# A decoder layer on one core: first weights through ACT's queue, gamma scaled on POOL, a scratch column for the shifted variance

## The chip, the core and the metric

The kernel runs on one core of a Trainium2 chip. A core has engines that run side by side, each on its own in-order stream of instructions: TensorE (PE; its weight loads are listed as PEld), VectorE (DVE), ScalarE (ACT), GpSimd (POOL) and SyncE (SP), which here only issues DMA transfers. ACT and POOL can issue transfers too, each on a queue of its own; an issue stands in the same stream as the engine's other instructions. Engines wait for each other and for transfers by semaphores.

The metric is device microseconds of one execution. The kernel before took 662.29 us in the median of three runs (661.71 to 663.59). All times inside an execution are counted from the first instruction that the profile shows.

## The reference

One decoder layer on x of 512 tokens by 1024 channels, float32:

```python
proj = h @ w_in[l]
q, k, v, p, g = jnp.split(proj, [...], axis=-1)
y_attn = moba_attention(q.reshape(hs), k.reshape(hs), v.reshape(hs), rel_bias) @ w_branch_attn[l]
y_pool = multiscale_pool(p, w_pool_group[l], pool_scale[l]) @ w_branch_pool[l]
gates = jax.nn.sigmoid(g.astype(jnp.float32)).astype(h.dtype).reshape(B, S, N_BRANCHES, D)
mixed = gates[:, :, 0] * y_attn + gates[:, :, 1] * y_pool
h = layer_norm(ALPHA * h + mixed @ w_out[l], ln1_g[l], ln1_b[l])
a, u = jnp.split(h @ w_ffn_in[l], 2, axis=-1)
a = causal_dwconv(a, conv_w[l], conv_b[l])
f = (jax.nn.gelu(a, approximate=False) * u) @ w_ffn_out[l]
h = layer_norm(ALPHA * h + f, ln2_g[l], ln2_b[l])
```

`layer_norm` is `(x - mean) * rsqrt(var + 1e-5) * gamma + beta` over the 1024 channels of a token.

## The kernel before, in words

**Three matmuls for one.** Every float32 operand is split into a high part (rounded to the format that TensorE multiplies at full rate) and the low remainder, and a product is three matmuls: high by high, high by low, low by high (`mm3`, L144 to L148). `split` (L63 to L68) does this: ACT copies the source into `hi` (L67), or another copy that is passed in does; then DVE subtracts, `lo = src - hi` (L68).

**The weight stream.** Weights come in chunks of 128 by 1024 (512 KB). `fetch` (L92) takes the next chunk: a DMA on SP's queue into one of three `wraw` buffers (L108), then the split into one of five pairs `whi`, `wlo`. The first chunk alone is fetched in two halves of 512 columns (`early`), each with its DMA and split, and between the halves the second half of the first tile of x is loaded. `weights(i)` runs three chunks ahead of the matmuls.

**The head.** ACT has a dummy activation (L164) so that its table is loaded early; POOL sets `eps_t`, which the dummy reads; DVE clears a tile, and TensorE runs eight dummy matmuls on it (`WARM`, L168). Meanwhile x, transposed, comes in eight tiles of 128 by 512 (`load_x`, L171), the first in two halves whose high parts are made by DVE (L65, `nc.vector.tensor_copy`). The first real matmuls are those of v (L240), 12 for each of the eight tiles of x; a weight chunk serves two of these tiles.

**The middle.** Then follow the other input projections with attention and pooling between them, the branch projections (for each of eight channel tiles `f`, POOL adds the two gated branches, `mt`, L437, and the sum is split into `mx_hi`, `mx_lo`), the output projection (`wo`), the first layer norm, and the gated MLP's input matmuls (`fi`).

**The end.** The MLP's output matmul is done as seven products of half-size blocks (Strassen-like; `product`, L664, in the order of `PRODUCTS`). Some products read weight sums, which a DMA from POOL's queue accumulates into `tw` (L134); two read plain weights (`wraw`, L128). The last products are followed by the second layer norm, one row tile of 128 tokens after the other: `scale_out` for tiles 0 and 1, `share_out` for 2, `finish` for 3.

**Layer norm.** `ln_rows` (L447) loads gamma and beta, each copied to all 128 partitions (one DMA of 1 MB on POOL's queue, L449), and ACT multiplies gamma by -0.5 in place (L450). It is called for the first norm (L454) and for the second (L709); there the tile takes the place of another one (`ra`) and two DMAs on SP's queue then write beta into rows of `out` (L711). `moments` (L470): DVE's per-256-column statistics `st` (six numbers each) are aggregated to mean and variance in `mv` (L472), ACT takes the square root of variance plus epsilon (L473), and DVE adds epsilon to the variance in place (L474). `centre` computes `(x - mean) * (-0.5 gamma)` (L485). `invert` makes `1/sqrt` with one Newton step from both (L479 to L481), and its result scales the row (L489 and ACT).

**Order.** The program is written in the order above, but the order of the instructions on each engine is chosen when the kernel is built, by a planner that works with estimated durations; it is fixed afterwards. `finish` pins part of its DVE instructions in the written order.

Of the kernel before, what the change touches and what calls it, by code (L numbers as in the profile page):

```python
# [10 lines left out]
AF = mybir.ActivationFunctionType  # L11
ALU = mybir.AluOpType
# [15 lines left out]
EPS = 1e-5  # L28
# [3 lines left out]
LEAD = 3  # L32
RING = 5
TMP = 4
WARM = 8
NKEEP = 12
NLATE = 4
KH = NF // 2
# [5 lines left out]
def layer_kernel(ctx: ExitStack, tc: tile.TileContext, xT, x, w_v, w_c, rel_bias, invcnt, w_group,  # L44
                 pscale, w_br, w_out, lnr, w_fi, convp, w_fo, out):
    nc = tc.nc
# [9 lines left out]
    def bank(name):  # L56
        return ps.tile([P, S], F32, tag="ps", name=name)
# [5 lines left out]
    def split(hi, lo, src, copy=None):  # L63
        if copy:
            copy(hi, src)  # L65
        else:
            nc.scalar.activation(hi, src, AF.Copy)  # L67
        nc.vector.tensor_tensor(lo, src, hi.bitcast(F32), op=ALU.subtract)  # L68
# [9 lines left out]
    chunks = [w_v[c] for c in range(4)]  # L78
# [13 lines left out]
    def fetch(pool=None, early=None):  # L92
        i = state["next"]
        state["next"] = i + 1
        if isinstance(chunks[i], tuple):
            ready[i] = fetch_fo(i, *chunks[i])
            return
        raw = wp.tile([P, D], F32, tag="wraw", name=f"wraw{i}", bufs=3)
        if pool is None:
            hi = wp.tile([P, D], F32R, tag="whi", name=f"whi{i}", bufs=RING)  # L100
            lo = wp.tile([P, D], F32R, tag="wlo", name=f"wlo{i}", bufs=RING)
        else:
            hi = pool.tile([P, D], F32R, name=f"whi{i}")
            lo = pool.tile([P, D], F32R, name=f"wlo{i}")
        parts = 2 if early else 1
        for c in range(parts):
            sl = slice(c * (D // parts), (c + 1) * (D // parts))
            nc.sync.dma_start(raw[:, sl], chunks[i][:, sl])  # L108
            split(hi[:, sl], lo[:, sl], raw[:, sl])
            if c == 0 and early:  # L110
                early()
        ready[i] = (hi, lo)
# [7 lines left out]
    def fetch_fo(i, name, c):  # L120
        sl = piece(c)
        n = sl.stop - sl.start
        step = {"T3": "=B11", "B11": "+B12", "T1": "+B22", "T2": "+B21", "T4": None}
        if name in step:
            raw = tw[:, sl]
        else:
            raw = wp.tile([P, D], F32, tag="wraw", name=f"wraw{i}", bufs=3)[:, :n]
            nc.sync.dma_start(raw, half(name, sl))  # L128
        hi = wp.tile([P, D], F32R, tag="whi", name=f"whi{i}", bufs=RING)[:, :n]
        lo = wp.tile([P, D], F32R, tag="wlo", name=f"wlo{i}", bufs=RING)[:, :n]  # L130
        split(hi, lo, raw)
        then = step.get(name)
        if then and then[0] == "+":
            nc.gpsimd.dma_start(raw, half(then[1:], sl), accum_op=ALU.add)  # L134
        elif then:
            nc.sync.dma_start(raw, half(then[1:], sl))
        return hi, lo

    def weights(i):
        while state["next"] <= min(i + LEAD, state["limit"]):  # L140
            fetch()
        return ready[i]
# [6 lines left out]

    def split3(v, a):  # L150
        return tuple(t.rearrange("p (a c) -> p a c", a=a) for t in v)

    xT_hi = act.tile([P, KT, S], F32R, tag="actT_hi", name="xT_hi")
    xT_lo = act.tile([P, KT, S], F32R, tag="actT_lo", name="xT_lo")
# [12 lines left out]
    wb_ = bank("warm_ps")  # L167
    for i in range(WARM):  # L168
        nc.tensor.matmul(wb_, warm[:, :P], warm, start=True, stop=True)
# [5 lines left out]
    for kt in range(KT):  # L175
        xr = aw.tile([P, S], F32, tag="tmp", name=f"xr{kt}", bufs=TMP)
        if kt == 0:
            load_x(kt, xr, slice(0, 256), nc.vector.tensor_copy)
            fetch(early=lambda: load_x(kt, xr, slice(256, 512), nc.vector.tensor_copy))
        else:  # L180
            load_x(kt, xr)
            if kt % 2 == 0:
                fetch()
# [44 lines left out]
    for kt in range(KT):  # L228
        wh, wl = split3(weights(kt // 2), 2)
        wh, wl = wh[:, kt % 2, :], wl[:, kt % 2, :]  # L230
        xs_ = [(xT_hi[:, kt, j * P:(j + 1) * P], xT_lo[:, kt, j * P:(j + 1) * P]) for j in range(NT)]
        last = kt == KT - 1
        if last:
            for j in range(NT):
                mm3(bs[j], xs_[j], (wh, wl), False, True)
                nc.scalar.activation(vv[:, j, :], bs[j], AF.Copy)
        else:
            for n, (a, b) in enumerate(((0, 0), (1, 0), (0, 1))):
                for j in range(NT):
                    nc.tensor.matmul(bs[j], xs_[j][a], (wh, wl)[b], start=kt == 0 and n == 0, stop=False)  # L240
# [55 lines left out]
    def in_tile(n):  # L296
        kind, j = order[n]
        wh, wl = split3(weights(C0 + n), KT)
        b = bank(f"{kind}{j}")
        for kt in range(KT):  # L300
            mm3(b, (wh[:, kt, :], wl[:, kt, :]), (xT_hi[:, kt, :], xT_lo[:, kt, :]), kt == 0, kt == KT - 1)
        if kind == "q":
            q_done(j, b)
        elif kind == "k":
            k_done(j, b)
        elif kind == "p":
            pool_in(j, b)
        elif len(gslot) < NKEEP:
            gslot[j] = gates[:, len(gslot), :]
            nc.vector.tensor_copy(gslot[j], b)  # L310
        else:
            gslot[j] = late[:, len(gslot) - NKEEP, :]
            nc.scalar.activation(gslot[j], b, AF.Sigmoid)
# [106 lines left out]
    for f in range(KT):  # L420
# [7 lines left out]
        for br in (1, 0):  # L428
            b = bank(f"br{f}_{br}")
            for k in range(4):  # L430
                src = (zT_hi[:, k, :], zT_lo[:, k, :]) if br else (oT_hi[:, k, :], oT_lo[:, k, :])
                mm3(b, (wh[:, 4 * br + k, :], wl[:, 4 * br + k, :]), src, k == 0, k == 3)
            t = bp.tile([P, S], F32, tag="m", name=f"m{f}_{br}", bufs=4)
# [13 lines left out]
    def ln_rows(r):  # L447
        t = hw.tile([P, 2, D], F32, tag="lnb", name=f"lnb{r}")
        nc.gpsimd.dma_start(t, bass.AP(tensor=lnr.tensor, offset=lnr.offset + r * D, ap=[[0, P], [D, 2], [1, D]]))  # L449
        nc.scalar.activation(t[:, 0, :], t[:, 0, :], AF.Copy, scale=-0.5)  # L450
        return t

    lnb = ln_rows(0)
    ypool = ctx.enter_context(tc.tile_pool(name="ypool", bufs=1, reuse_waits="tile"))  # L454
    ytiles = [ypool.tile([P, S], F32, name=f"y{j}") for j in range(2)]
# [4 lines left out]
    st = const.tile([P, NT, 4, 6], F32, name="st")  # L460
# [9 lines left out]
    def moments(i):  # L470
        mu, var = mv[:, i, 0:1], mv[:, i, 1:2]
        nc.vector.bn_aggr(mv[:, i, :], st[:, i].rearrange("p a b -> p (a b)"))  # L472
        nc.scalar.activation(rstd[:, i, 0:1], var, AF.Sqrt, bias=eps_t)  # L473
        nc.vector.tensor_scalar(var, var, EPS, None, op0=ALU.add)  # L474
        return mu, var

    def invert(i, var, pin=lambda ins: ins):
        r, t = rstd[:, i, 0:1], rstd[:, i, 1:2]
# [14 lines left out]
    def scale_out(i):  # L493
        mu, var = moments(i)
        centre(i, slice(0, D), mu)
        r = invert(i, var)
        nc.scalar.activation(xs[:, i, :], xs[:, i, :], AF.Copy, scale=r)
        nc.gpsimd.dma_start(out[i * P:(i + 1) * P, :], xs[:, i, :], accum_op=ALU.add)

    def share_out(i):  # L500
        mu, var = moments(i)
        centre(i, slice(0, D), mu)
        r = invert(i, var)
        nc.scalar.activation(xs[:, i, right], xs[:, i, right], AF.Copy, scale=r)
        rescale(i, left, r)
        nc.gpsimd.tensor_tensor(xs[:, i, right], xs[:, i, right], lnb[:, 1, right], op=ALU.add)

    def finish(i):
        pin = tc.keep_in_program_order
        mu, var = moments(i)  # L510
        pin(centre(i, right, mu))
        r = invert(i, var, pin)
        nc.scalar.activation(xs[:, i, rest], xs[:, i, rest], AF.Copy, scale=r)
        pin(centre(i, left, mu))
        nc.gpsimd.tensor_tensor(xs[:, i, rest], xs[:, i, rest], lnb[:, 1, rest], op=ALU.add)
        pin(rescale(i, left, r))
        pin(rescale(i, most, r))
# [106 lines left out]
    for j in range(RING, 2 * NF):  # L624
        hb[j] = bank(f"fi{j}")
        fi_mm(j, hb[j], slice(0, S))
        if j % 2:
# [3 lines left out]
            if f % 2 == 0 and f >= 6 and f < 6 + 2 * NC:  # L631
                c = f // 2 - 3
# [74 lines left out]
    gather(3, S, D, bank_a[1], 1, False, False)  # L707
    product(5, bank_d, False)
    lnb = ln_rows(2)  # L709
    for i in range(2):  # L710
        nc.sync.dma_start(out[i * P:(i + 1) * P, :], lnb[:, 1, :])  # L711
# [89 lines left out]
```

## Time and profile before

| | us |
|---|---|
| median of three runs | 662.29 |
| the profiled execution, whole | 663.32 |
| its span, first to last instruction | 661.6 |
| TensorE busy in it | 649.4 |
| VectorE busy | 384.4 |
| ScalarE busy | 285.9 |
| GpSimd busy | 89.3 |
| DMA, mean | 127 GB/s, 83.70 MB |

How to read the rows that follow. A row of the timeline has the start and the duration in us, the engine (with a q behind it: the issue of a DMA or another sequencer instruction), the line, the operation, what it writes and reads, and how many were merged; in brackets is how long its engine had been idle before it, and what ended that. A row of the chain of waits has start, duration and what the chain ran through; a DMA there lasts from issue to landing. A row of the groups has the count, then busy us, mean ns of one, and idle us before them. A row of the waits has who waited for whom, the sum in us, how often and the longest. A row of DMA issues has the count, the size of each, and the median us to landing. A row of a stretch has its bounds and length, busy us of each engine in the order PE, PEld, DVE, ACT, POOL, the granted clock, the share of the DMA engines' time, and GB/s. A busy TensorE is not a TensorE at its peak, since the ends of matmuls are modelled and overlap the next ones.

### The profile page before, as it was taken

Reading aid. Unit: us, or ns where it says so; the run is one execution under the profiler, and the core shown is the slowest. Engines: PE = TensorE matmul, PEld = TensorE weight load, DVE = VectorE, ACT = ScalarE, POOL = GpSimd, SP = SyncE. Lnnn points to the kernel's source line nnn. Section 1 sums busy time; section 2 is a strip of 40 time slices with the busy share of each in tenths; the row PEclk is TensorE's granted clock in tenths of the full one; section 3 lists DMA queues with packets and bytes.
Section 4 is the critical chain, followed back from the end, with each engine's and each line's share of the span. In section 5 each row is a group of like instructions: output and inputs, shape, how many; then the busy total and the mean of one; then the engine's idle time right before and its main releaser. Section 6 shows DMA issues by size and latency. Waiting matters only on the chain.

```text
span 661.6 us, 8020 instructions
## 1 busy us (share of the span) xinstructions
PE 649.4 (98%) x3083; PEld 538.8 (81%) x3083; DVE 384.4 (58%) x559; ACT 285.9 (43%) x395; POOL 89.3 (14%) x137
## 2 busy tenths in 40 slices
PE   8999999999999999999999999999999999999994
PEld 6888787877888888889988888888888888888874
DVE  5556665554532675398456344443534548788596
ACT  5646556675422332232443333333323236555452
POOL 0705261211000124002100000000000001124002
PEclk9999999999999999999999999999999999999998
DMA  8643222222322227208942222233233334989905
GB/s 285 215 150 118 80 79 80 73 74 79 96 95 96 93 98 291 91 1 292 251 157 97 96 95 96 95 100 101 99 97 97 104 100 97 211 188 203 261 1 127
DMA packets 24918, 83.70 MB, mean 127 GB/s; under 512 B 3240, under 2 KB 3496, under 8 KB 24624
## 3 DMA queue, kind: packets, MB, share of 16 engines
q1 hardware_dynamic: 19312, 63.77, 29.1%
q0 software_dynamic: 5280, 18.90, 13.2%
q8 instruction: 24, 0.39, 0.2%
q10 hardware_dynamic: 288, 0.52, 0.2%
q14 instruction: 14, 0.11, 0.1%
HBM read 80.01 MB, written 3.17 MB: 126 GB/s over the span
## 4 chain that ended last, share of the span: by engine, by line
PE 77%; issue 10%; DMA 4%; POOL 4%; DVE 3%; ACT 1%; POOLq 0%; DVEq 0%; SPq 0%; ACTq 0%
PE fi L147 11%; PE fi L146 11%; PE fi L148 11%; PE g L146 4%; PE g L147 4%; PE g L148 4%; PE v L240 3%; PE wo L146 2%; PE br L147 2%; PE br L146 2%; PE wo L147 2%; PE wo L148 2%; PE br L148 2%; POOL tw L134 2%; PE ob L372 1%
## 5 line engine op out<-in xcount | busy, mean ns | idle before, releaser
L68 DVE TENSOR_TENSOR wlo<-wraw,whi 128x1024 fp32r<-128x1024 f32 (+1 forms) x105 | 134.3, 1284 | 119.8 <-ACT whi L67 117.9
L67 ACT ACTIVATE whi<-wraw 128x1024 fp32r<-128x1024 f32 (+1 forms) x105 | 109.0, 1041 | 187.4 <-PE fi L147 84.0
L147 PE MATMUL fi<-hT_lo,whi 128*128 128x512 f32 (+1 forms) x392 | 143.8, 367 | 0.0
L148 PE MATMUL fi<-hT_hi,wlo 128*128 128x512 f32 (+1 forms) x392 | 143.8, 367 | 0.0
L146 PE MATMUL fi<-hT_hi,whi 128*128 128x512 f32 (+1 forms) x392 | 143.5, 368 | 0.0
L148 PEld LDWEIGHTS fi<-hT_hi,wlo 128*128 128x128 f32 x392 | 73.9, 189 | 12.3
L147 PEld LDWEIGHTS fi<-hT_lo,whi 128*128 128x128 f32 x392 | 73.9, 189 | 12.0
L146 PEld LDWEIGHTS fi<-hT_hi,whi 128*128 128x128 f32 x392 | 73.6, 189 | 12.2
L134 POOL DMA_DIRECT2D tw<-in_w_fo x18 | 15.8, 906 | 269.9 <-DVE wlo L68 269.9
L146 PE MATMUL g<-xT_hi,whi 128*128 128x512 f32 x128 | 50.3, 393 | 0.0
L148 PE MATMUL g<-xT_hi,wlo 128*128 128x512 f32 x128 | 49.9, 390 | 0.0
L147 PE MATMUL g<-xT_lo,whi 128*128 128x512 f32 x128 | 49.8, 389 | 0.0
L67 ACT ACTIVATE whi<-tw 128x1024 fp32r<-128x1024 f32 (+1 forms) x30 | 29.4, 983 | 25.4 <-PE fi L147 11.3
L578 DVE TENSOR_TENSOR fT<-y,fi 128x512 f32<-128x512 f32 x22 | 15.1, 687 | 40.0 <-PE fi L148 39.2
L68 DVE TENSOR_TENSOR wlo<-tw,whi 128x1024 fp32r<-128x1024 f32 (+1 forms) x30 | 33.3, 1126 | 8.6 <-ACT whi L67 8.4
L577 ACT ACTIVATE y<-y 128x512 f32<-128x512 f32 x22 | 13.9, 632 | 43.0 <-DVE y L576 43.0
L148 PEld LDWEIGHTS g<-xT_hi,wlo 128*128 128x128 f32 x128 | 24.0, 188 | 5.1
L146 PEld LDWEIGHTS g<-xT_hi,whi 128*128 128x128 f32 x128 | 24.0, 188 | 5.0 <-issue 0.2
L147 PEld LDWEIGHTS g<-xT_lo,whi 128*128 128x128 f32 x128 | 24.0, 188 | 4.8
L345 POOL TENSOR_SCALAR pp<-pp,rs 128x128 f32<-128x128 f32 (+3 forms) x32 | 21.8, 698 | 37.7 <-PE g L148 18.4
L146 PE MATMUL wo<-whi,mx_hi 128*128 128x512 f32 x64 | 25.0, 390 | 0.0
L148 PE MATMUL wo<-whi,mx_lo 128*128 128x512 f32 x64 | 24.9, 389 | 0.0
(202 smaller groups left out, 1169.7 us busy)
## 6 DMA issues: line engine op xcount, KB each, us to landing
wraw<-in_w_fi SPq DMA_DIRECT2D x44, 512.0 KB, 3.3
wraw<-in_w_c SPq DMA_DIRECT2D x28, 512.0 KB, 3.4
tw<-in_w_fo POOLq DMA_DIRECT2D x20, 512.0 KB, 7.6
tw<-in_w_fo SPq DMA_DIRECT2D x10, 512.0 KB, 3.9
wraw<-in_w_fo SPq DMA_DIRECT2D x10, 512.0 KB, 5.2
wraw<-in_w_br SPq DMA_DIRECT2D x8, 512.0 KB, 3.3
wraw<-in_w_out SPq DMA_DIRECT2D x8, 512.0 KB, 3.4
strip<-F_d POOLq DMA_DIRECT2D x8, 256.0 KB, 3.5
```

The lines of the kernel that those rows point to most:

```text
L67: nc.scalar.activation(hi, src, AF.Copy)
L68: nc.vector.tensor_tensor(lo, src, hi.bitcast(F32), op=ALU.subtract)
L134: nc.gpsimd.dma_start(raw, half(then[1:], sl), accum_op=ALU.add)
L146: nc.tensor.matmul(out_, wh, ah, start=start, stop=False, **kw)
L147: nc.tensor.matmul(out_, wh, al, start=False, stop=False, **kw)
L148: nc.tensor.matmul(out_, wl, ah, start=False, stop=stop, **kw)
L240: nc.tensor.matmul(bs[j], xs_[j][a], (wh, wl)[b], start=kt == 0 and n == 0, stop=False)
L345: nc.gpsimd.tensor_scalar(pp[:, offs[i]:offs[i] + n], pp[:, offs[i]:offs[i] + n], rs[:, i:i + 1], 1.0, op0=ALU.mult, op1=ALU.mult)
L372: nc.tensor.matmul(b[e * DH:(e + 1) * DH, kb * P:], vv[:, kb, h * DH:(h + 1) * DH], PTs[h][:, toff[kb]:toff[kb] + n], start=kb == 0, stop= ...
L577: nc.scalar.activation(y, y, AF.Gelu)
L578: nc.vector.tensor_tensor(fT[:, j, :], y, u, op=ALU.mult)
```

## The change

Four things are changed:

1. One dummy matmul fewer (`WARM` 8 to 7).
2. The two halves of the first weight chunk are loaded by DMAs on ACT's queue, no longer SP's. The high part of the first half is made by two engines: DVE copies columns 0 to 191 and ACT columns 192 to 511. The second half is split as before.
3. Gamma is multiplied by -0.5 on POOL, no longer on ACT, at both calls of `ln_rows`.
4. Variance plus epsilon goes into the first number of the row tile's statistics, which are not read again after the aggregate, no longer over the variance itself.

```diff
-WARM = 8
+WARM = 7
...
-            nc.sync.dma_start(raw[:, sl], chunks[i][:, sl])
-            split(hi[:, sl], lo[:, sl], raw[:, sl])
+            (nc.scalar if early else nc.sync).dma_start(raw[:, sl], chunks[i][:, sl])
+            split(hi[:, sl], lo[:, sl], raw[:, sl], fast if early and c == 0 else None)
...
+    def fast(hi, src):
+        for copy, c in ((nc.vector.tensor_copy, slice(0, 192)), (first_copy, slice(192, 512))):
+            copy(hi[:, c], src[:, c])
+
+    def first_copy(hi, src):
+        nc.scalar.activation(hi, src, AF.Copy)
...
-        nc.scalar.activation(t[:, 0, :], t[:, 0, :], AF.Copy, scale=-0.5)
+        nc.gpsimd.tensor_scalar(t[:, 0, :], t[:, 0, :], -0.5, None, op0=ALU.mult)
...
-        nc.vector.tensor_scalar(var, var, EPS, None, op0=ALU.add)
-        return mu, var
+        shifted = st[:, i, 0, 0:1]
+        nc.vector.tensor_scalar(shifted, var, EPS, None, op0=ALU.add)
+        return mu, shifted
```

## The prediction

> **What bounds the kernel now.** I read the page's busy shares first, then who TensorE waited for, then the first 14 us, the last 60 us, and the gamma steps.
>
> ```profile
> span 661.6 us, 8020 instructions
> PE 649.4 (98%) x3083; PEld 538.8 (81%) x3083; DVE 384.4 (58%) x559; ACT 285.9 (43%) x395; POOL 89.3 (14%) x137
> ...
> PE warm_ps L169 <- DVE warm L166: 1.3, 1, 1.3
> PE v L240 <- ACT whi L67: 0.7, 1, 0.7
> PE fod L147 <- DVE wlo L68: 0.7, 1, 0.7
> ```
>
> TensorE is the bound: 649.4 of 661.6 us busy, and the three longest of its waits sum to 2.7 us. The change removes no matmul but one dummy, so it can gain only before the first matmul, after the last one, in the 0.7 us ahead of `fod`, and where matmuls run slowly. The head:
>
> ```profile
> 0.81 1.28 ACT L164 ACT_TABLE_LOAD   x1 [0.81 <-PEq L793]
> 1.25 0.42 SPq L108 DMA_DIRECT2D wraw<-in_w_v  x1
> 1.25 3.63 DMA wraw<-in_w_v
> 1.27 3.59 PE L169 MATMUL warm_ps<-warm 128*128 128x512 bf16 x8 [1.27 <-DVE warm L166]
> 2.10 0.20 ACT L164 ACTIVATE dummy<-eps_t 128x1 f32<-128x1 f32 x1
> 3.05 0.29 DVE L65 CAST xT_hi<-xr 128x256 fp32r<-128x256 f32 x1 [1.84 <-DMA xr<-in_xT]
> 4.91 0.63 ACT L67 ACTIVATE whi<-wraw 128x512 fp32r<-128x512 f32 x1 [2.60 <-DMA wraw<-in_w_v]
> 5.59 1.22 PE L240 MATMUL v<-whi,xT_hi 128*128 128x512 f32 x2 [0.73 <-ACT whi L67]
> 6.62 1.05 PE L240 MATMUL v<-whi,xT_lo 128*128 128x512 f32 x2
> 7.47 1.05 PE L240 MATMUL v<-whi,xT_hi 128*128 128x512 f32 x2
> 9.18 0.62 PE L240 MATMUL v<-whi,xT_lo 128*128 128x512 f32 x2
> 9.97 1.06 ACT L67 ACTIVATE whi<-wraw 128x1024 fp32r<-128x1024 f32 x1 [1.35 <-DMA wraw<-in_w_v]
> 11.02 1.07 PE L240 MATMUL v<-whi,xT_lo 128*128 128x512 f32 x4
> 11.92 1.07 PE L240 MATMUL v<-wlo,xT_hi 128*128 128x512 f32 x4
> ```
>
> (Start, duration, engine.) The first half chunk of weights is issued at 1.25, lands 3.63 us later, takes 0.63 us on ACT, and the first real matmul starts at 5.59; x was ready at 3.34. Matmuls start (7.47-6.62)/2 = 0.425 us apart until about 9.17, and (11.92-11.02)/4 = 0.225 apart after it. The stretch 5.59 to 9.17 thus runs at about half speed, and costs 3.58 x (1 - 0.225/0.425) = 1.68 us.
>
> **Part 1, first weights on ACT's queue, split by two engines.** An issue holds SP for 0.42 us (second row); the weights were second. On ACT they can go at 0.81, where that engine's stream began: 0.44 us earlier, if the issue precedes the table load (ready without a wait, while the dummy waits for `eps_t`). Transit to landing is unknown for this queue: the lower end is x's first slice, 3.05-0.82 = 2.23 us with nothing ahead; the upper is 3.63, this transfer behind that slice. I take 3.63, since the same 384 KB must move by then. Then the split: ACT's rows give 0.63 us for 512 columns and 1.06 for 1024, 0.84 ns each, so 320 columns cost 0.63 - 192 x 0.00084 = 0.47. DVE's 192 columns cost less than its 0.29 us for 256, and run beside ACT's. That saves 0.16. First matmul: 5.59 - 0.44 - 0.16 = 4.99, **0.60 us earlier**. The low end of the gain is below nothing (table load first, a rival below); the high end is 5.59-4.43 = 1.16, because the warm-up then stands in the way: one dummy fewer ends it at 4.86 - 0.43 = 4.43. That removed dummy saves nothing by itself and leaves an idle gap of 0.56 instead of 0.73.
>
> Also moved: SP loses two issues, so the x tiles and the second weight chunk go about 2 x 0.42 = 0.84 us sooner. That chunk's `whi` (11.03) has cover: TensorE reaches it after the eight matmuls of the last two rows, near 12.8. With the second half chunk issued late on ACT, say at 2.73, cover remains: landing 3.63 us later and split in 0.63, it would be ready at 7.0; it is used after twelve matmuls, about 9.18 + 4 x 0.225 = 10.1. I take the slow stretch to shift along with its start.
>
> The Trainium skill (DMA: Bandwidth & Descriptors, "Queues, rings and completion order") says that each DMA engine alternates between the queues that have work. By that rule x, now next on SP, shares with the weights, and these end after 512 KB rather than 384; this trace never has both queues at work, so it cannot confirm it. What that gives is a rival below.
>
> **Part 2, gamma on POOL.**
>
> ```profile
> L345 POOL TENSOR_SCALAR pp<-pp,rs 128x384 f32<-128x384 f32 x8 | 8.6, 1069 | 0.0
> L345 POOL TENSOR_SCALAR pp<-pp,rs 128x512 f32<-128x512 f32 x8 | 6.5, 816 | 0.0
> ...
> 251.82 0.54 POOL L449 DMA_DIRECT2D lnb<-in_lnr  x1
> 253.91 1.28 POOL L437 TENSOR_TENSOR mt<-m,m 128x512 f32<-128x512 f32 x1 [1.56 <-DVE m L434]
> 262.31 2.14 POOL L437 TENSOR_TENSOR mt<-m,m 128x512 f32<-128x512 f32 x1 [7.12 <-DVE m L434]
> 265.14 0.69 DVE L68 TENSOR_TENSOR mx_lo<-mt,mx_hi 128x512 fp32r<-128x512 f32 x1 [1.85 <-ACT mx_hi L67]
> 278.23 1.37 DVE L466 SCALAR_TENSOR_TENSOR xs<-xs,wo 128x512 f32<-128x512 f32 x2 [8.83 <-PE wo L148]
> ...
> DMA to landing us min/median/max: 8.2/9.2/10.6
> ```
>
> ACT loses two passes over 1024 columns (about 1.05 us each); POOL gains two, of 2 x 0.816 = 1.6 to 1.069 x 1024/384 = 2.9 us. They also make POOL wait for a landing of up to 10.6 us (last row). The first could hold the two mixing adds behind it: landing 251.8+10.6 = 262.4, scaled by 265.3, then adds, ACT, DVE: the last `mx_lo` moves from 265.8 to at most about 271. The last twelve `wo` matmuls that need it end when DVE resumes at about 278.2, so start near 275.5: hidden.
>
> The second:
>
> ```profile
> 613.95 1.06 ACT L450 ACTIVATE lnb<-lnb 128x1024 f32<-128x1024 f32 x1 [4.25 <-DMA lnb<-in_lnr]
> 632.18 1.06 ACT L67 ACTIVATE whi<-tw 128x1024 fp32r<-128x1024 f32 x1 [0.36 <-PE fod L148]
> ...
> 613.88 1.73 SPq L711 DMA_DIRECT2D out<-lnb  x2
> 618.37 3.74 SPq L128 DMA_DIRECT2D wraw<-in_w_fo  x3
> ...
> tw<-in_w_fo POOLq DMA_DIRECT2D x5, 512.0 KB, 10.7
> out<-lnb SPq DMA_DIRECT2D x2, 512.0 KB, 9.4
> ...
> 618.37 8.18 DMA wraw<-in_w_fo
> 633.48 0.50 PE fod L147
> ```
>
> ACT stood 4.25 us for gamma; behind it were `sd_hi`, `whi`, and so the weight buffer that SP refills at 618.37, whose landing at 626.55 leads to the 0.7 us stall at 633.48. Freed, ACT could let that load go at 613.88+1.73 = 615.6. But the two 512 KB beta stores of SP are ahead in the same queue and take 9.4 us to land, to about 625. The load's end follows them, whenever it is issued. So the ends are 0 and 0.7; I take **0**, as the row of 8.18 us says that this load queued rather than travelled. On POOL the `tw` additions behind gamma can be held until 613.9 + 2.9 = 616.8; the first then lands near 616.8+10.7 = 627.5, and ACT reads that piece at 632.18: hidden with 4.7 us left.
>
> **Part 3, the dead column.**
>
> ```profile
> 653.58 0.26 DVE L472 BATCH_NORM_AGGREGATE mv<-st 128x2 f32<-128x24 f32 x1
> 653.87 0.30 ACT L473 ACTIVATE rstd<-mv,eps_t 128x1 f32<-128x1 f32 x1 [1.77 <-DVE mv L472]
> 654.20 0.15 DVE L474 TENSOR_SCALAR mv<-mv 128x1 f32<-128x1 f32 x1 [0.36 <-ACT rstd L473]
> 654.27 0.74 DVE L485 SCALAR_TENSOR_TENSOR xs<-xs,mv,lnb 128x512 f32<-128x512 f32 x1
> ```
>
> In the last row tile, epsilon is added in place, so DVE idles 0.36 us until ACT has read the variance, with the centring, inverse and final scaling queued behind and no matmul left. Written elsewhere, the add follows the aggregate at once; the square root, done at 654.17, is still ahead of the reciprocal, which comes after 0.74 us of centring. Gain **0.36 us**; bounds 0 and 0.36. The other seven row tiles lie under matmuls.
>
> **Sum.** 0.60 + 0 + 0.36 = 0.96 us. The profiled execution took 663.32, 1.72 around its span and 1.03 above the median 662.29; on it the sum gives 662.36, on the median 661.33: **661.3 us**.
>
> **Rivals.**
> - *The slow stretch ends early* (chance 0.27). In the trace full speed came 3.58 us after the end of the idle gap (5.59), not after the first dummy (1.27). If the first weights land so early that the gap closes or is too short to count, 1.27+3.58 = 4.85 could end it, and the 1.68 us go too: 0.60+1.68+0.36 = 2.64, **659.7**. Against it: I leave 0.56 us of gap; and TensorE would want the second chunk at 12.8-2.3 = 10.5, before the `whi` at 11.03 if that comes no sooner. The Trainium skill (TensorE: Matmul & The Clock Gate, "Part 1: The HAM clock gate") says that full clock follows a window of about 3.4 us of sustained activity, and that the windows run freely; the 3.58 agrees, and a drifting start of windows would also vary from run to run.
> - *The stall goes as well* (0.15): 0.96+0.7 = 1.66, **660.6**. For it, 2.8 us earlier issue; against, the beta stores ahead.
> - *Shared engines* (0.13). The extra 128 KB ahead, at the rate just after (row below), cost 0.42 us and eat the earlier issue: 0.16-0.42+0.44+0.36 = 0.54, **661.8**.
> - *Slower: the issue stands behind ACT's table load* (0.10). ACT's first activation ends at 2.30; weights issued there instead of at 1.25 lose 1.05, less 0.16 and 0.36: **662.8**. It decides from an issue later than 1.25+0.16+0.36 = 1.77. For it: the dummy is ahead in the program; against: it needs `eps_t` first.
>
> ```profile
> 4.86:5.59 0.73, 0.00 (x0) 0.00 (x0) 0.31 (x2) 0.63 (x1) 0.00 (x0) 1.00 0.92 313
> ```
>
> (128 KB at the last column's 313 GB/s is 0.42 us.)
>
> **Numbers.** The forecast has 0.30, an unforeseen order of the work the last 0.05. The range reaches from below the early-clock case (with the stall gone as well it would be 659.0) to the table-load case: 659.0 to 662.9; the forecast's own bounds are 660.8 (1.16 + 0.36) to 662.1 (the split's 0.16 alone). A change of 0.3%, 2.0 us, is about what a measurement here can tell: faster means under 660.3. That takes nearly all of the early clock, a third of the stall case and some of the forecast's high gains and new orders: 0.40. Slower means above 664.3, which only a new order could bring or the table load with a longer slow stretch: 0.06. The rest, 0.54, is the same.
>
> **What would show it.** The first weight issue on ACT at 0.81 and the first real matmul near 5.0 confirm part 1; an issue after 2.30 is the slower rival. Starts 0.425 apart until about 8.6 confirm the shifted slow stretch; 0.225 from before 6 is the first rival. A wait of `fod` for `wlo` of 0.7 us in the sixth product confirms the load's queueing; its absence is the second. No idle time of DVE between the last aggregate and the epsilon addition confirms part 3. Any new wait of TensorE behind `mx` or `tw` refutes the cover on POOL. The prediction is wrong if it is not these rows but others that move.

## The result and the profile after

| | before | after |
|---|---|---|
| median, us | 662.26 (22 runs, 661.38 to 664.59) | 660.57 (22 runs, 659.38 to 663.26) |
| ratio after to before | | 0.9972, interval 0.9962 to 0.9981 |
| the profiled execution, whole | 663.32 | 659.63 |
| its span | 661.6 | 657.8 |
| first real matmul starts | 5.59 | 4.87 |
| thirteenth real matmul starts | 10.10 | 7.70 |
| first `fi` matmul to TensorE's end | 349.02 | 348.07 |
| TensorE's end to the span's end | 8.99 | 8.56 |

The median fell by 1.69 us; the sum of the prediction was 0.96. The two profiled spans differ by more, 3.8 us: 2.4 in the first ten microseconds, 0.95 behind the first `fi` matmul, 0.43 after the last matmul. The 2.4 are mostly the luck of two executions: the head alone, in e1_head below, brings 0.21 by the medians.

The page of the changed kernel, with the busy shares and the chain by engine, and then TensorE's longest waits, from the view of the waits (who waited for whom, sum in us, times, longest).

```profile
span 657.8 us, 8016 instructions
PE 647.0 (98%) x3082; PEld 537.6 (82%) x3082; DVE 384.9 (59%) x560; ACT 284.7 (43%) x393; POOL 95.5 (15%) x139
...
PE 94%; DVE 2%; POOL 2%; ACT 1%; DMA 1%; issue 0%; DVEq 0%; ACTq 0%; POOLq 0%
```

```profile
PE warm_ps L176 <- DVE warm L173: 1.2, 1, 1.2
PE zb L146 <- ACT difh L67: 0.5, 2, 0.3
PE v L247 <- ACT whi L158: 0.5, 1, 0.5
```

TensorE is still the bound. The wait of `fod` for `wlo` that stood in this list is gone, and no wait on `mx` or `tw` has come. POOL has 6.2 us more work (89.3 before), ACT 1.2 less.

The timeline of the changed kernel, the head:

```profile
0.79 0.41 ACTq L108 DMA_DIRECT2D wraw<-in_w_v  x1
1.24 1.28 ACT L171 ACT_TABLE_LOAD   x1 [1.24 <-PEq L801]
1.25 3.17 PE L176 MATMUL warm_ps<-warm 128*128 128x512 bf16 x7 [1.25 <-DVE warm L173]
3.80 0.29 DVE L65 CAST xT_hi<-xr 128x256 fp32r<-128x256 f32 x1 [2.60 <-DMA xr<-in_xT]
4.30 0.47 ACT L158 ACTIVATE whi<-wraw 128x320 fp32r<-128x320 f32 x1 [1.56 <-DMA wraw<-in_w_v]
4.47 0.25 DVE L155 CAST whi<-wraw 128x192 fp32r<-128x192 f32 x1
4.87 0.69 PE L247 MATMUL v<-whi,xT_hi 128*128 128x512 f32 x2 [0.45 <-ACT whi L158]
5.40 0.63 PE L247 MATMUL v<-whi,xT_lo 128*128 128x512 f32 x2
5.87 0.62 PE L247 MATMUL v<-whi,xT_hi 128*128 128x512 f32 x2
```

and the chain of waits, where the transfer lasts from issue to landing:

```profile
0.79 3.48 DMA wraw<-in_w_v
```

The weights are issued at 0.79, ahead of the table load, and land after 3.48 us. The first slice of x is later than it was: its cast starts at 3.80 instead of 3.05. ACT's part of the split took 0.47 us as worked out, and the matmul follows at 4.87. From the second pair on, matmuls start (5.87-5.40)/2 = 0.235 us apart: full speed almost at once, where before it came at 9.18.

The same view around the last loading of gamma and beta (SP, POOL and ACT):

```profile
611.43 3.84 POOL L457 TENSOR_SCALAR lnb<-lnb 128x1024 f32<-128x1024 f32 x1 [5.15 <-DMA lnb<-in_lnr]
615.23 1.81 POOL L134 DMA_DIRECT2D tw<-in_w_fo  x2
611.36 0.89 SPq L719 DMA_DIRECT2D out<-lnb  x2
612.66 5.77 SPq L128 DMA_DIRECT2D wraw<-in_w_fo  x3
622.11 1.06 ACT L67 ACTIVATE whi<-wraw 128x1024 fp32r<-128x1024 f32 x1 [5.48 <-DMA wraw<-in_w_fo]
```

and the view of the tensor `out`, here its two stores of beta:

```profile
DMA to landing us min/median/max: 6.6/7.0/7.4
```

The late load is issued 1.3 us behind the first store of beta, where before it was 4.5 us (613.88, 618.37), and ACT reads it at 622.11 instead of 626.66. The stores themselves land after 7.0 us; before it was 9.4. And POOL, which waited 5.15 us for gamma and then scaled it for 3.84, issues its last two additions at 615.23, behind SP's load.

The tail:

```profile
650.24 0.26 DVE L479 BATCH_NORM_AGGREGATE mv<-st 128x2 f32<-128x24 f32 x1
650.54 0.30 ACT L480 ACTIVATE rstd<-mv,eps_t 128x1 f32<-128x1 f32 x1 [1.77 <-DVE mv L479]
650.54 0.15 DVE L482 TENSOR_SCALAR st<-mv 128x1 f32<-128x1 f32 x1
650.61 0.74 DVE L493 SCALAR_TENSOR_TENSOR xs<-xs,mv,lnb 128x512 f32<-128x512 f32 x1
651.27 0.16 DVE L487 RECIPROCAL rstd<-rstd 128x1 f32<-128x1 f32 x1
```

The addition of epsilon now starts at 650.54, together with the square root; the 0.36 us of idle time is gone from DVE.

### The profile page after: what moved, and what is told of

Its sections match the earlier page's. It is cut to its first block, busy times and chain, and to the rows that moved or that the text cites. A ratio compares the mean times of both kernels' runs of the same rounds, so it can differ in the third digit from the quotient of the medians.

```text
span 657.8 us, 8016 instructions
## 1 busy us (share of the span) xinstructions
PE 647.0 (98%) x3082; PEld 537.6 (82%) x3082; DVE 384.9 (59%) x560; ACT 284.7 (43%) x393; POOL 95.5 (15%) x139
## 4 chain that ended last, share of the span: by engine, by line
PE 94%; DVE 2%; POOL 2%; ACT 1%; DMA 1%; issue 0%; DVEq 0%; ACTq 0%; POOLq 0%
PE fi L148 12%; PE fi L147 12%; PE fi L146 12%; PE g L146 4%; PE g L148 4%; PE g L147 4%; PE v L247 3%; PE wo L147 2%; PE br L148 2%; PE br L147 2%; PE wo L148 2%; PE wo L146 2%; PE br L146 2%; PE fod L148 2%; PE foa L148 2%; PE foa L147 2%
## 5 line engine op out<-in xcount | busy, mean ns | idle before, releaser
L444 POOL TENSOR_TENSOR mt<-m,m 128x512 f32<-128x512 f32 x8 | 11.2, 1394 | 96.0 <-DVE m L441 79.3
```

Of the source, the lines that this page charges most:

```text
L444: nc.gpsimd.tensor_tensor(mt, m[1], m[0], op=ALU.add)
```

## The experiments

Three batches, each with its own runs of the kernel before: 662.15 in the first (e1 to e4), 662.03 in the second, on another chip (e5, e9 to e11), 662.21 in the third (e6, e7, e12, e13). Line numbers in diffs are left out. Parts are counted as in the prediction: the head, gamma, the dead column.

**The three parts alone.** e1_head has the changed head, and of the rest nothing:

```diff
-WARM = 8
+WARM = 7
...
-            nc.sync.dma_start(raw[:, sl], chunks[i][:, sl])
-            split(hi[:, sl], lo[:, sl], raw[:, sl])
+            (nc.scalar if early else nc.sync).dma_start(raw[:, sl], chunks[i][:, sl])
+            split(hi[:, sl], lo[:, sl], raw[:, sl], fast if early and c == 0 else None)
```

> The kernel before with parts 1 and 2 of the change alone (one dummy matmul fewer, first weights on ACT's queue, the first half split by two engines). Theory: the changed kernel's 1.69 us between the medians (662.26 to 660.57) are the sum of three terms that do not touch each other: 0.72 us at the head (first real matmul at 5.59 before, 4.87 after), 0.66 us of stall in the sixth product, 0.33 us in the last layer norm. Then this kernel gains about 0.7 us, to 661.55, and its profile keeps the stall of about 0.66 us ahead of fod. Rival (clock): the head also lets full speed come earlier in most runs, as in the one profile of the changed kernel, where matmuls were 0.23 us apart from the second pair on; then the head alone gains 1.5 us or more, to 660.7 or less, and the other parts give little.

Measured: 661.94, ratio 0.9992 (0.9981 to 1.0003). By the medians 0.21 us, and no difference that can be told. The timeline of its head:

```profile
3.71 0.29 DVE L65 CAST xT_hi<-xr 128x256 fp32r<-128x256 f32 x1 [2.50 <-DMA xr<-in_xT]
4.03 0.42 DVE L68 TENSOR_TENSOR xT_lo<-xr,xT_hi 128x256 fp32r<-128x256 f32 x1
4.38 0.25 DVE L155 CAST whi<-wraw 128x192 fp32r<-128x192 f32 x1
4.09 0.47 ACT L158 ACTIVATE whi<-wraw 128x320 fp32r<-128x320 f32 x1 [1.33 <-DMA wraw<-in_w_v]
4.78 0.91 PE L247 MATMUL v<-whi,xT_hi 128*128 128x512 f32 x2 [0.34 <-DVE whi L155]
```

Here the matmul waits for DVE, not for ACT. ACT's 320 columns could be read from 4.09 on; DVE's 192 start at 4.38, since x's late slice stands ahead of them in DVE's order. DVE's part ends at 4.63, ACT's at 4.56, so that what the split saves on ACT is partly given back there.

e2_gamma scales gamma on POOL, and nothing else is changed:

```diff
-        nc.scalar.activation(t[:, 0, :], t[:, 0, :], AF.Copy, scale=-0.5)
+        nc.gpsimd.tensor_scalar(t[:, 0, :], t[:, 0, :], -0.5, None, op0=ALU.mult)
```

> The kernel before with gamma scaled on POOL alone. Theory (ACT's wait was the cause of the stall): fod no longer waits for wlo in the sixth product, and the gain is 0.66 us, to 661.6. Rival, as the prediction had it (the weight load queues behind the beta stores whenever it is issued): the stall of 0.66 us stays and the time is that of before, 662.26.

Measured: 660.70, ratio 0.9979 (0.9967 to 0.9991): 1.45 us, most of what the whole change brings. TensorE's wait of `fod` for `wlo` is gone from its profile. So the part that the prediction put at nothing is the one that carries the result.

e3_column writes variance plus epsilon elsewhere:

```diff
-        nc.vector.tensor_scalar(var, var, EPS, None, op0=ALU.add)
-        return mu, var
+        shifted = st[:, i, 0, 0:1]
+        nc.vector.tensor_scalar(shifted, var, EPS, None, op0=ALU.add)
+        return mu, shifted
```

> The kernel before with the shifted variance in the dead column alone. Theory: from the last TensorE instruction to the end of the span 8.99 us become about 8.65, and the time falls by 0.33 us, to 661.9, below what five rounds can tell from nothing. Rival: the square root is late next (DVE's reciprocal waits for it), and the stretch after the last matmul stays 8.99.

Measured: 661.68, ratio 0.9994 (0.9983 to 1.0004), 0.47 by the medians, too little to tell by the time alone. In the profile the stretch from TensorE's end to the span's end went from 8.99 to 8.65 us, 0.34 less; the wait of `fod` is still there, with 0.9. The three parts add up to 0.21 + 1.45 + 0.47 = 2.13, against 1.69 for the whole; the intervals cover the difference.

**Why the load lands earlier.** In e2_gamma two things move at once: ACT no longer waits for gamma, so that the weight buffer comes free and SP issues the late load some 3 us sooner; and POOL does wait, so that its last two additions (512 and 256 KB) are issued some 3 us behind the stores, not ahead of them. The first theory (A): the load's earlier issue is enough. The second (B): the additions' delay is. The next two kernels keep the first and take away the second. e4_act_late is the changed kernel with the second gamma on ACT, but behind ACT's splits of the chunks, so that no split waits for gamma and POOL isn't held:

```diff
-            nc.scalar.activation(hi, src, AF.Copy)
+            state["act"] = nc.scalar.activation(hi, src, AF.Copy)
...
-        nc.gpsimd.tensor_scalar(t[:, 0, :], t[:, 0, :], -0.5, None, op0=ALU.mult)
+        def scale():
+            nc.scalar.activation(t[:, 0, :], t[:, 0, :], AF.Copy, scale=-0.5)
+
+        if r:
+            with tc.issue_after(state["act"].ins):
+                scale()
+        else:
+            scale()
```

> The changed kernel, with gamma scaled on ACT again, the second time queued behind ACT's last split that is traced before it (a piece of the seventh product's weights), so that ACT does not stand still for gamma's landing and POOL does not hold its two last tw additions until it. Theory A (ACT's wait was the cause): no stall ahead of fod, the time is the changed kernel's 660.57 within 0.3 us. Theory B (it is the held tw additions that gave the weight load its share of the DMA engines): the stall of about 0.66 us is back, and the time is about 661.2.

Measured: 661.75, ratio 0.9995 (0.9981 to 1.0010). Its timeline and its waits:

```profile
609.82 1.76 POOL L134 DMA_DIRECT2D tw<-in_w_fo  x2 [1.73 <-DVE wlo L68]
614.51 0.89 SPq L726 DMA_DIRECT2D out<-lnb  x2
615.50 4.74 SPq L128 DMA_DIRECT2D wraw<-in_w_fo  x3
627.29 1.06 ACT L67 ACTIVATE whi<-wraw 128x1024 fp32r<-128x1024 f32 x1 [8.85 <-DMA wraw<-in_w_fo]
```

```profile
PE fod L147 <- DVE wlo L68: 1.5, 2, 1.0
```

The load is issued 1.0 us behind the first store, as in the changed kernel, and is still not read until 627.29, 11.8 us later. The wait is back, twice. Theory A falls.

e5_pool_late leaves gamma on POOL, but behind the last addition:

```diff
-            nc.gpsimd.dma_start(raw, half(then[1:], sl), accum_op=ALU.add)
+            state["add"] = nc.gpsimd.dma_start(raw, half(then[1:], sl), accum_op=ALU.add)
...
+        def scale():
+            nc.gpsimd.tensor_scalar(t[:, 0, :], t[:, 0, :], -0.5, None, op0=ALU.mult)
+
+        if r:
+            with tc.issue_after(state["add"].ins):
+                scale()
+        else:
+            scale()
```

> The changed kernel with gamma's second scaling on POOL queued behind the last tw addition, so that neither ACT nor the tw additions wait for gamma's landing. Theory B (the two tw additions, 768 KB, held on POOL until gamma has landed leave the DMA engines to the weight load): they are issued near 608 again, the first of the three late weight loads lands about 12.8 us after gamma, as in the kernel before, the head kernel and the column kernel (12.7 to 13.8), and the stall ahead of fod is back with 0.4 to 1.5 us; time about 661.5. Theory A (it is enough that ACT is free): load about 10 us after gamma, no stall, 660.6.

Measured: 661.49, ratio 0.9987 (0.9977 to 0.9997). The same two views:

```profile
607.84 1.76 POOL L134 DMA_DIRECT2D tw<-in_w_fo  x2 [1.74 <-DVE wlo L68]
611.56 0.88 SPq L726 DMA_DIRECT2D out<-lnb  x2
612.53 5.72 SPq L128 DMA_DIRECT2D wraw<-in_w_fo  x3
624.99 1.06 ACT L67 ACTIVATE whi<-wraw 128x1024 fp32r<-128x1024 f32 x1 [8.54 <-DMA wraw<-in_w_fo]
```

```profile
PE fod L147 <- DVE wlo L68: 1.2, 2, 1.0
```

The same again: the load is out at 612.53, and its first reader starts 12.5 us later. With the additions ahead, the early issue buys nothing at this place. By the times alone it could not be told, since this interval reaches into that of the changed kernel (0.9962 to 0.9981); the profile decides.

e9_hold tries the other half alone: the kernel before, ACT still scaling gamma, with POOL made to wait for the landing by a copy of one column, so that the additions go behind it.

```diff
+    seen = hw.tile([P, 1], F32, name="seen")
...
+        if r:
+            nc.gpsimd.tensor_copy(seen, t[:, 1, :1])
```

> The kernel before with one POOL instruction more, a copy of a single column of beta behind gamma's and beta's second load; gamma stays on ACT, which waits for it as before, and the order on ACT, DVE, SP and TensorE is the same. POOL now holds its two last tw additions until the landing. Theory B: the first late weight load lands about 10 to 11 us after gamma although it is issued 4.5 us after it, the stall of 0.4 to 0.9 us goes or shrinks to under 0.3, and the time is 0.7 to 1.4 us below the kernel before. Theory A: the stall stays, and the time is that of before.

Measured: 667.84, ratio 1.0089 (1.0072 to 1.0107), and the time is no answer, since the loss isn't at this place: the groups of instructions by form show that all the `fi` matmuls of 512 columns in the MLP are slower (count, busy us, mean ns). Its profile has no wait of `fod` left, but its load is read 13.46 us behind the stores' issue, no sooner than in the kernel before (12.78); with the `fod` matmuls slower too (398 ns against 392), that can't be put down to the hold. First e9_hold's row, then the same row with the copy into a tile that the kernel already has, which is e12_hold_same_tiles:

```profile
L147 PE MATMUL fi<-hT_lo,whi 128*128 128x512 f32 x312 | 123.2, 395 | 0.0
```

```profile
L147 PE MATMUL fi<-hT_lo,whi 128*128 128x512 f32 x312 | 121.4, 389 | 0.0
```

```diff
+        if r:
+            nc.gpsimd.tensor_copy(dummy, t[:, 1, :1])
```

> The kernel with the holding POOL copy again, but the copied column goes into the dummy tile that exists already, so that no tile moves. The earlier form had no stall left, yet took 667.84 us, with the 512-column matmuls of the MLP's input 395 ns long instead of 389 and 0.233 us apart instead of 0.227. Theory (the one new column moved the tiles behind it, and TensorE's pace hangs on where they lie): those matmuls are 389 ns again, there is no stall ahead of fod, and the time is 0.7 to 1.4 us below before, 660.7 to 661.4. Rival (the copy or the hold itself slows the matmuls): 395 ns and about 668 again.

Measured: 662.26, ratio 0.9993 (0.9980 to 1.0006). The slower matmuls came with the new tile of one column and went with it. And the hold, in the timeline and the waits of e12_hold_same_tiles:

```profile
613.36 1.76 POOL L134 DMA_DIRECT2D tw<-in_w_fo  x2 [0.30 <-issue]
612.83 1.28 SPq L713 DMA_DIRECT2D out<-lnb  x2
617.33 3.73 SPq L128 DMA_DIRECT2D wraw<-in_w_fo  x3
625.58 1.06 ACT L67 ACTIVATE whi<-wraw 128x1024 fp32r<-128x1024 f32 x1 [6.89 <-DMA wraw<-in_w_fo]
```

```profile
PE fod L147 <- DVE wlo L68: 0.9, 1, 0.9
```

The additions now go 0.5 us behind the first store, but 4 us ahead of the load, which ACT holds back as before. The wait stays at 0.9. So theory B in its simple form, that a hold of any length is enough, falls too. A hold of some 3 us, as POOL's scaling gives it, with ACT still waiting for gamma, was not tried.

**Are the stores in the way?** The prediction had said that the load's end follows the two stores of beta. e10_stores_late takes the kernel before and issues them behind the last loads:

```diff
-            nc.sync.dma_start(raw, half(name, sl))
+            state["load"] = nc.sync.dma_start(raw, half(name, sl))
...
-    for i in range(2):
-        nc.sync.dma_start(out[i * P:(i + 1) * P, :], lnb[:, 1, :])
+    with tc.issue_after(state["load"].ins):
+        for i in range(2):
+            nc.sync.dma_start(out[i * P:(i + 1) * P, :], lnb[:, 1, :])
```

> The kernel before with one edit: on SP's queue the two beta stores (1 MB) stand behind the three late weight loads instead of ahead of them. The prediction's step that the load queues behind these stores: the first load then lands within about 6 us of its issue instead of 8.2 to 9.3, before TensorE needs it, and the stall goes though ACT waits for gamma and the tw additions are not held; time 0.7 to 1.4 us below before. Rival (the tw additions alone slow it): it lands as late as before, and the stall stays.

Measured: 660.61, ratio 0.9973 (0.9962 to 0.9984). The timeline:

```profile
617.29 3.74 SPq L128 DMA_DIRECT2D wraw<-in_w_fo  x3
621.08 0.90 SPq L712 DMA_DIRECT2D out<-lnb  x2
622.89 1.06 ACT L67 ACTIVATE whi<-wraw 128x1024 fp32r<-128x1024 f32 x1 [4.23 <-DMA wraw<-in_w_fo]
```

Issued as late as before, at 617.29, the load is read 5.6 us after its issue, where it was 8.3 before, and no wait of `fod` is left. That part of the prediction holds: the load queued behind the stores. e11_after_stores_late does the same to the changed kernel:

> The changed kernel with the same edit of the stores. Its profile had no stall left in the sixth product, so theory B gives the changed kernel's time, 660.57 within 0.3 us. Rival: in runs other than the profiled one the changed kernel still stalls there at times; then the median falls below 660.4 and the spread narrows.

Measured: 660.13, ratio 0.9961 (0.9946 to 0.9976), its five runs between 659.41 and 660.34. That is what the rival asked for, a changed kernel that still stalls in some executions; but the interval reaches into that of the changed kernel, so the times don't show it.

The table has all profiles at this place (us; the first four columns of numbers are starts from the timelines; "landing" is the median of the two stores; the last but one is the stretch from the first `fi` matmul to TensorE's end, which holds whatever is lost here).

| kernel | stores issued | late load issued | last two additions | ACT reads the load | stores' landing | stretch | waits of `fod` |
|---|---|---|---|---|---|---|---|
| before | 613.88 | 618.37 | 610.38 | 626.66 | 9.4 | 349.02 | 0.7 |
| e1_head | 611.32 | 615.81 | 608.06 | 624.12 | 9.4 | 348.85 | 0.4 |
| e3_column | 612.43 | 616.92 | 609.31 | 626.21 | 9.7 | 349.65 | 0.9 |
| e12_hold_same_tiles | 612.83 | 617.33 | 613.36 | 625.58 | 9.1 | 349.63 | 0.9 |
| e9_hold (slower matmuls) | 617.22 | 621.72 | 617.75 | 630.68 | 9.6 | 355.18 | 0 |
| e4_act_late | 614.51 | 615.50 | 609.82 | 627.29 | 9.2 | 350.26 | 1.5 |
| e5_pool_late | 611.56 | 612.53 | 607.84 | 624.99 | 9.8 | 349.91 | 1.2 |
| e2_gamma | 612.59 | 613.75 | 615.73 | 622.36 | 6.7 | 348.07 | 0 |
| after | 611.36 | 612.66 | 615.23 | 622.11 | 7.0 | 348.07 | 0 |
| e7_warm4 | 614.40 | 615.43 | 617.99 | 626.08 | 7.2 | 348.07 | 0 |
| e6_warm8 | 612.59 | 613.68 | 615.38 | 624.44 | 7.2 | 349.16 | 0.8 |
| e10_stores_late | 621.08 | 617.29 | 608.58 | 622.89 | 5.3 | 348.07 | 0 |
| e11_after_stores_late | 618.95 | 613.13 | 615.69 | 619.14 | 8.0 | 348.07 | 0 |
| e13_both | 619.42 | 614.44 | 615.03 | 619.47 | 8.5 | 348.07 | 0 |

In the first seven rows the additions are out ahead of the stores, or 0.5 us behind the first of them: the stores take 9.1 to 9.8 us to land, and the load is read 12.8 to 13.8 us after the stores' issue, whether it was itself issued 1 us behind them (e4, e5) or 4.5. In the next four the additions follow 2.8 to 3.9 us behind: the stores land in 6.7 to 7.2, and the load is read 9.8 to 11.9 after. Where the stores are taken out of the way, the load is read 5.0 to 6.0 us after its own issue. So the load ends behind the stores, as predicted, and the stores end sooner if the additions leave them alone. Whether the load also gains from being ahead of the additions is not told apart by these runs.

Two more readings of the table. The cover is thin: e6_warm8 has the new order and still a wait of 0.8. Its stores took no longer than e7_warm4's, and its load was read 11.85 us behind their issue, against 11.68; but gamma and beta, which the stores wait for, took 10.0 us to come (602.59 to 612.59, from their load's issue to the stores') where in e7_warm4 they took 9.1 (605.30 to 614.40). And in four profiles that have both the stores and the additions ahead of a load held by ACT (the first four rows) the stretch is 0.78 to 1.58 us above the 348.07 of undisturbed ones, 1.22 on the mean: what is lost there is more than the one profile's 0.7 of idle time, and this agrees with the 1.45 and 1.42 us that e2_gamma and e10_stores_late gain.

**The clock at the head.** In the profile of after TensorE was at full speed from the second pair of matmuls on. Was that the change? e6_warm8 closes the gap between the dummies and the first real matmul, e7_warm4 opens it.

```diff
-WARM = 7
+WARM = 8
```

> The changed kernel with eight dummy matmuls instead of seven. In ten profiles so far TensorE stood idle between the dummies and the first real matmul for 0.60 to 0.73 us twice, and ran at half speed until 8.6 or 9.2; with a gap of 0.45 or less (eight profiles) full speed came by 5.9. Theory (the gap decides): eight dummies end at about 4.85, where the first weights are ready, the gap is under 0.2, full speed comes by 6 in every run, the time is the changed kernel's 660.57 or up to 0.3 below, and the runs above 661.7 (4 of its 22) become rarer. Rival (chance decides when full speed comes): no difference in median or spread.

Measured: 660.50, ratio 0.9959 (0.9945 to 0.9973); no gap left, full speed from 5.50 on, and none of its ten runs above 661.7, where four of the changed kernel's 22 lie. With `WARM = 4` instead:

> The changed kernel with four dummy matmuls. They end near 3.15, the gap is about 1.7 us. Theory (the gap decides): half speed until about 3.6 us after the first real matmul in every run, near 8.5, and the median is 1.2 to 1.7 us above the changed kernel, 661.8 to 662.3. Rival (chance, or the time since the first dummy, decides): full speed by 6 in the profile, and 660.6.

Measured: 661.71, ratio 0.9988 (0.9974 to 1.0002). The timeline of its head:

```profile
1.25 1.89 PE L176 MATMUL warm_ps<-warm 128*128 128x512 bf16 x4 [1.25 <-DVE warm L173]
4.77 1.22 PE L247 MATMUL v<-whi,xT_hi 128*128 128x512 f32 x2 [1.64 <-ACT whi L158]
5.79 1.05 PE L247 MATMUL v<-whi,xT_lo 128*128 128x512 f32 x2
...
9.21 1.05 PE L247 MATMUL v<-wlo,xT_hi 128*128 128x512 f32 x2
10.06 1.49 PE L247 MATMUL v<-whi,xT_hi 128*128 128x512 f32 x4
```

The first real matmul is where it was, at 4.77, but pairs start 0.85 us apart up to 10.06: half speed for 5.3 us, longer than the 3.6 or so that was expected. The median came out just under the range that was expected, 661.8 to 662.3. The same view of e2_gamma, which has the old head:

```profile
4.25 0.63 ACT L67 ACTIVATE whi<-wraw 128x512 fp32r<-128x512 f32 x1 [1.95 <-DMA wraw<-in_w_v]
4.93 1.00 PE L240 MATMUL v<-whi,xT_hi 128*128 128x512 f32 x2
5.77 0.63 PE L240 MATMUL v<-whi,xT_lo 128*128 128x512 f32 x2
```

Full speed from 5.77, with the head of before. The idle gap ahead of the first real matmul sorts the profiles, not the head: the three longest gaps have the three latest starts of full speed, of fourteen profiles.

| gap, us | profiles | full speed from |
|---|---|---|
| 1.64 | e7_warm4 | between 10.1 and 11.4 |
| 0.73 | before | 9.2 |
| 0.60 | e4_act_late | 8.6 |
| 0.45 to 0.06 | after, e11, e10, e3, e1, e5, e2, e13 | 5.3 to 7.3 |
| none | e6, e9, e12 | 5.5 to 7.1 |

The gap isn't all: with less than 0.1 us of it (e2, e13) or none, full speed still came anywhere between 5.5 and 7.3. Of the six profiles with the old head (before, e2, e3, e9, e10, e12) five have it by 7.1: the profile of before was the exception. The slow stretch that the prediction kept was that of this one execution.

The Trainium skill (TensorE: Matmul & The Clock Gate, "Part 1: The HAM clock gate") has full clock follow a window of about 3.4 us of sustained activity, with windows that run freely. The rows agree as far as they go. In before and e4_act_late full speed came 3.6 us after the first real matmul (5.59 to 9.18, 5.03 to 8.58), in e7_warm4 5.3 us or more after it; in the eleven profiles with a gap of 0.45 or less it came 4.0 us (e5_pool_late) to 6.0 us (e13_both) after the first dummy, and in none sooner. If the gap alone decides whether the dummies count, the limit lies between 0.45 and 0.60 us here.

**The best of both.** e13_both is the changed kernel with the stores behind the loads and eight dummies:

> The changed kernel with the beta stores behind the weight loads and eight dummies. If stores and gap each take away a cause of slow runs, the median is 660.1 or below and no run lies above 661; if they do nothing, 660.57.

Measured: 659.93, ratio 0.9952 (0.9934 to 0.9970), the lowest median of all, 0.64 us under that of the changed kernel. The intervals overlap, so the times alone don't separate it from the changed kernel; its profile has no wait of `fod`, and 0.06 us of gap at the head.

## Why the prediction was right, and where not

The range and the direction were right: 660.57 lies in 659.0 to 662.9, faster by 0.28 (0.19 to 0.38) %, at the edge of what the prediction called telling. The likeliest sum was 0.7 us short, and 660.57 lies below the forecast's own bounds, 660.8 to 662.1. The sum is made of other terms than those that happened: the head was put too high and the stall too low, and that the two errors partly offset each other is luck.

- **The stall ahead of `fod`: the step that failed.** The prediction took 0 for it, because "The load's end follows them, whenever it is issued". The sentence is right: e4_act_late and e5_pool_late issue the load early and lose the gain, e10_stores_late takes the stores away and gets it. What failed is the step from there to 0. The stores' own end was taken as fixed, at about 625, and it isn't: it moves from 9.4 us to 7.0 with POOL's additions out of the way. The prediction had that hold in its hands ("On POOL the `tw` additions behind gamma can be held until 613.9 + 2.9 = 616.8"), and counted it as a possible harm only, not as 768 KB less traffic beside the stores. The rival "the stall goes as well" had 0.15 and the right time, 660.6, for a reason that is not the one that the runs show: the earlier issue of the load.
- **The size of that stall** was put at 0.7, from one profile's idle time. It costs 1.22 on the mean of four profiles, and 1.45 by the times of e2_gamma.
- **The head: two terms mis-sized.** The issue went at 0.79, as said (0.81), and ACT's part of the split took 0.47, as said; together they were to bring 0.60. e1_head brings 0.21 (the interval reaches from -0.2 to 1.3). All profiles of the head, taken together, say where the rest went (starts in us, the mean in brackets):

  | head | profiles | weights issued | ACT reads them | from issue to that | x's first slice read | first real matmul | from ACT's start to that |
  |---|---|---|---|---|---|---|---|
  | old | 6 | 1.23 to 1.25 | 3.86 to 4.91 (4.34) | 2.62 to 3.66 (3.10) | 2.93 to 3.12 | 4.54 to 5.59 (5.02) | 0.68 to 0.69 (0.68) |
  | new | 8 | 0.79 to 0.81 | 4.01 to 4.30 (4.16) | 3.21 to 3.51 (3.36) | 3.61 to 3.96 | 4.68 to 5.03 (4.84) | 0.52 to 0.90 (0.68) |

  The prediction took 3.63 us of transit, from one profile, for both queues. That was a long one: on the mean the weights need 0.26 us more on the new path than on the old, and of 0.44 us of earlier issue 0.18 is left when ACT reads them. x's first slice is read 0.73 us later on the mean (3.76 against 3.04), and later in every profile with the new head than in any with the old. Both are what the rival "shared engines" describes, which had put its price at 0.42. The split was to save 0.16, since DVE's columns "run beside ACT's"; on the mean it saves nothing, since they stand behind x's late slice in DVE's order, and in e1_head, e4_act_late and e11_after_stores_late the matmul waits for DVE. The first matmul is 0.18 us earlier on the mean, which agrees with e1_head's 0.21. The Trainium skill (DMA: Bandwidth & Descriptors, "Issuing engines are not separate DMA queues") says that transfers of all engines interleave on the same DMA engines, and that a second issuer saves only the time of issuing. These rows agree: 0.44 of issue gained for the weights, of which 0.18 is left at their reading, and 0.73 lost for x.
- **The slow stretch.** The prediction's forecast let it move along with the start, and gave 0.27 to its end. In after's profile it hardly appeared, but the same holds of most profiles with the old head; little of the 1.69 in the medians can come from it. The rival's condition, a gap too short to count, is borne out by the gaps above, but the old head mostly met it too. e6_warm8 against e7_warm4 in one batch, 660.50 against 661.71, shows what the gap is worth.
- **The tail: right.** 0.36 predicted; 0.43 in after's profile, 0.34 in e3_column's, and the row of the addition moved ahead of the square root's end, as the prediction asked.
- **POOL's cover: right.** The last additions were issued by 617.0 (predicted 616.8), and TensorE waits neither for `tw` nor for `mx`. Each scaling was put at 1.6 to 2.9 us; the first took 2.78 and came behind the mixing adds, not ahead of them, the second took 3.84, and the cover bore it. (The 10.6 us allowed for gamma's landing was a store's; gamma's load took 9.2.)
- **The slower rival** is refuted: the issue at 0.79 is ahead of the table load at 1.24.

What stays open: whether the late load gains by being ahead of the additions in time, apart from the faster stores; whether a hold of POOL's additions as long as this one would do without freeing ACT; and how often each kernel's executions have the early full speed, as each has one profile.

## What to carry to other kernels

When a transfer queues behind others, ask what sets the end of those others, and list every transfer on other queues that the change moves out of that window or into it: a hold on an idle engine can be the gain. A term read from one profiled execution (a first start, a slow stretch, a stall of 0.7 us) is one draw; a part run alone, with several runs beside it, tells its size. Stores whose data nobody waits for belong behind the loads that somebody does wait for: that one edit alone brought 0.9973 (0.9962 to 0.9984), as much as the whole change.

## What the runs showed of the hardware that was not expected

One more tile of one column, written once, in e9_hold made the 128x512 `fi` matmuls 395 ns instead of 389 and the kernel 5.8 us slower (667.84 against 662.03); with the copy going to a tile that was there already, both were gone (389 ns, 662.26). The new tile moves those allocated after it in its pool; that the operands' place in memory is what slows the matmuls is the likely reading, but no run moved only them. An idle gap of 0.60 us behind the dummies went with half speed up to 8.6 us, one of 0.45 with full speed by 5.4 in one profile (after) and by 6.4 in another (e11).
